# Scores of differential attention with keys as [high, low] on all 128 rows of TensorE

## The chip, the cores and the metric

The kernel runs on one core of a Trainium2 chip. The metric is the device time of one execution in microseconds (us), lower is better. Of the kernel before, three runs are shown: 2396.42, 2398.08 and 2400.06 us, median 2398.08 us. All matrix products are of float32 data; most are made as three products of `float32r` parts, a high part (the value rounded to that type) and a low part (what is left).

## The reference

One layer for a prompt of 1024 tokens with 16 meta tokens ahead of it, and for a sample of 8 streams of 16 new tokens each. A common in-projection feeds a retention branch (4 heads) and a differential attention branch (8 heads); both are gated and merged, and a feed-forward part with a final norm follows. What the change touches is the score product of the attention and the state update of the sample in the retention:

```python
def diff_softmax_mix(q, k, v, bias, mask, lam):
    s = jnp.einsum('bqhcd,bkhcd->bchqk', q, k) * (DIFF_DH ** -0.5) + bias
    s = jnp.where(mask, s, NEG_INF)
    p = jax.nn.softmax(s, axis=-1)
    a = p[:, 0] - lam * p[:, 1]
    return jnp.einsum('bhqk,bkhe->bqhe', a, v)
...
S_new = exp(lg * L) * Sf + jnp.einsum('bmhd,bmhe->bhde', kf * k_dec, vf)
```

Here `c` counts the two maps of a head, each with 64 channels (`DIFF_DH`), so that a score is a sum over 64 products.

## The kernel before, in words

**Stages.** A: norm, transposes and the first values (0 to about 45 us). B: retention, four heads, with dense products of the in-projection between its short products (to about 536 us). C: differential attention, eight heads, with the dense products of gates, of the next head's keys and queries, and at its end of the retention branch, between its short products (about 536 to 1280 us). D to F: the attention branch, the output projection and the feed-forward part (to the end at 2397 us).

**The scores (`scores`, L870 to L929).** For each block b of 128 queries and each of the two maps, the keys up to the block's end (144 to 1040 columns) are cut into one to three pieces. A piece is two products into one PSUM tile `psc` (two buffers, tag "m"): at L910 the queries `Q[:, m]` are the weights of 128 rows, 64 of the high part and 64 of the low part, against `K[:, m]`, which holds the high part of the keys twice; at L911 the 64 rows of the high queries alone stand against the 64 rows `KL` of the low keys. VectorE then adds the bias and takes the maximum in one instruction (L913), which frees the tile. So 224 pieces in all, 28 per head.

**Keys and queries (`task_kq`, L742 to L812).** For each head and each of three chunks of tokens ScalarE copies the keys out of PSUM (L754) and makes the two high halves (L755, L756); GpSimd copies each to the other 64 rows (L758, L759) and makes the low halves (L760, L762). Of the queries ScalarE makes the high halves (L781, L782) and VectorE the low ones (L785, L789) on the other 64 rows of the same tile.

**The sample's state (`load_kv` and L655 to L665).** For each retention head, eight products of 48 rows (16 tokens, three pairings of high and low) update the states of the streams; their operands come by DMA into `KV`.

**Order.** TensorE's program is written out by hand, and in stage C that of the other engines too. A planner (`Stream`, `weave`, `merge`) keeps a clock of TensorE's planned time: a short step is followed by dense steps of `C_RATIO` times its length; what other engines do is put into their program when the clock says that it should be ready (`LAT`), and a step that needs it waits by the clock ("at") while dense steps go on. The scores of a block wait for `rdy_kq`, which is set at L767 (keys: after four GpSimd steps of 1300 ns and 1500 ns) and L777 (queries: after 2200 ns). All DMAs go out on SyncE's queue.

Of the kernel before, what the change touches and what calls it, by code (L numbers as in the profile page):

```python
# [33 lines left out]
# of the 16 gate tiles, those computed beside heads 0..6 (the last stands beside head 7)  # L34
# [4 lines left out]
# ns that the other engines take, as the order of the program in attention supposes  # L39
T_LOAD, T_RAW = 3600, 5850  # L40
LAT = {
    "k": 1500, "kp": 1300, "q": 2200, "v": 6550, "max": 900, "exp": 900, "mix": 1300, "ah": 1050, "al": 1250,
# [4 lines left out]
# ns of two blocks' scores and of two blocks' values on TensorE  # L47
# [7 lines left out]
def nm(c):  # L55
    """Columns of chunk c without the meta tokens: (offset in the chunk, first, last of 1152)."""
    lo, hi = CH[c]
    o = NM if c == 0 else 0
    return o, lo + o - NM, hi - NM
# [3 lines left out]
def tile_kernel(ctx, tc, I, O):  # L63
# [41 lines left out]
    def rstd(small, ss, n, eps, name, mul=1.0):  # L105
        """(ss * mul + eps)^-0.5 on [:, n]; eps a number or a tile of the same shape."""
# [10 lines left out]
    class Stream:  # L117
        """Tasks (name, split, body) of dense products, issued step by step; a task's weights are asked for while
        the task before it runs. A step of 0 ns is one that has to wait for steps outside the stream.
        now is TensorE's time as far as the program stands. With defer, what another engine does at the end of  # L120
        a chain is put into the program only when the chain should have got there: each engine goes through its
        part of the program in order."""
# [47 lines left out]
        def run(self, ns):  # L170
            """Steps of ns in all, or as far as they go; the time they take."""
            done = 0
            while done < ns:
                t = self.step()
                if t == 0:
                    break
                done += t
            return done

        def until(self, name):  # L180
            """Through the end of the named task."""
            while self.name == name or any(n == name for n, _, _ in self.todo):
                t = self.step()
                assert t or self.name != name and all(n != name for n, _, _ in self.todo), (name, self.name)
# [3 lines left out]
    def split_w(pool_, src, name, sfx="", eng=None, raw_pool=None, wait=0):  # L188
        """A 4 KB-per-partition weight tile as two float32r parts."""
# [14 lines left out]
    # DRAM scratch  # L204
# [10 lines left out]
    # =====================================================================  # L215
    # In-projection: x^T in two float32r parts stays on chip
    # =====================================================================
# [7 lines left out]
    def tok_rows(b):  # L225
        """Block b: -1 is the meta tokens, 0..7 the prompt, 8 the sample; rows of x_all."""
# [7 lines left out]
    # Dense products run as one stream of tasks, split into steps of three matrix products, so that the  # L234
    # steps can stand between the short products of retention and attention. A step yields its time in ns.
    def dense_c(w, X, c, o, evac, name):
        """Chunk c of one 128-column tile of w^T x^T: evac(c, ps)."""
# [12 lines left out]
    def dense_x(w, evac, name, meta, ready=lambda c: True):  # L250
        """All of the tile, where ready(c) says that what the chunk overwrites has been read."""
# [5 lines left out]
    def dense_v(hs, evac, name):  # L257
        """256 columns of x @ w_in, tokens on partitions: evac(b, n, rows) per block."""
# [26 lines left out]
    def weave(main, ratio):  # L285
        """Steps of main with dense ones between them. Apart from its time, a step of main is ("at", t): wait
        until t by the stream's clock; or ("for", f): dense steps until f()."""
# [17 lines left out]
    def merge(*parts):  # L305
        """Steps of several parts (total ns, steps) side by side, each in its measure, those that wait behind."""
# [66 lines left out]
    # values of the attention heads 2r, 2r+1 (rows, as they are returned)  # L373
# [66 lines left out]
    # bytes of phase A go to what phase B writes late  # L440
# [5 lines left out]
    KV = pl.tile([3 * NQ, ND // 2, 384], R, name="KV", tag="kv")  # L446
# [13 lines left out]

    def side_tables():
        """Rows of the relative bias shifted by one per query, and lambda: for phase C."""
# [75 lines left out]
    def retention(r):  # L538
# [14 lines left out]
        def front(b):  # L553
            """The block's decayed scores, keys, values and queries, all but scores to come in two parts."""
# [35 lines left out]
        def load_kv(i):  # L590
            """Keys and values of four streams as 48 rows: [high, low, high] of the values, [high, high, low] of
            the keys."""
# [53 lines left out]
        # sample streams  # L646
# [24 lines left out]
    def gated(r):  # L671
        """Gated output of the head, transposed."""
# [52 lines left out]
    # the meta keys' 16 rows of probabilities and values: [high, low, high] and [high, high, low]  # L725
# [7 lines left out]
    Q = pc.tile([P, 2, NP], R, name="Q", tag="Q", bufs=1)  # L733
# [3 lines left out]
    # steps of a head that stand in the program: blocks of scores; "keys": the sample's keys are read  # L737
    seen = {h: set() for h in range(DH)}
    # its chunks of queries and keys that do
    done = {h: set() for h in range(DH)}  # L740

    def task_kq(h):  # L742
        def body_k(w):
            def evac_k(c, ps):
                if c == 0:
                    K = pc.tile([P, 2, NM + NP], R, name=f"K{h}", tag="K")
                    KL = pc.tile([P, NM + NP], R, name=f"KL{h}", tag="KL")
                    keys[h] = (K, KL)
                    load(KC[:, :, 0:PAST], I["cache_kT"][h])
                K, KL = keys[h]  # L750
# [7 lines left out]
                    lambda: nc.gpsimd.tensor_copy(K[64:128, 0, lo:hi], kf[0:64, lo:hi]),  # L758
                    lambda: nc.gpsimd.tensor_copy(K[0:64, 1, lo:hi], kf[64:128, lo:hi]),  # L759
                    lambda: nc.gpsimd.tensor_tensor(  # L760
                        KL[0:64, lo:hi], kf[0:64, lo:hi], K[0:64, 0, lo:hi].bitcast(F), op=ALU.subtract),
                    lambda: nc.gpsimd.tensor_tensor(  # L762
                        KL[64:128, lo:hi], kf[64:128, lo:hi], K[64:128, 1, lo:hi].bitcast(F), op=ALU.subtract),
# [3 lines left out]
                rdy_kq[h, "k", c] = G.now + 4 * LAT["kp"] + LAT["k"]  # L767
# [7 lines left out]
        def evac_q(c, ps):  # L775
# [5 lines left out]
            nc.scalar.activation(Q[0:64, 0, lo:hi], ps[0:64, :n], AF.Copy, scale=0.125)  # L781
            nc.scalar.activation(Q[64:128, 1, lo:hi], ps[64:128, :n], AF.Copy, scale=0.125)  # L782

            def low():
                nc.vector.scalar_tensor_tensor(  # L785
                    Q[64:128, 0, lo:hi], ps[0:64, :n], 0.125, Q[0:64, 0, lo:hi].bitcast(F),
                    op0=ALU.mult, op1=ALU.subtract,
                )
                nc.vector.scalar_tensor_tensor(  # L789
                    Q[0:64, 1, lo:hi], ps[64:128, :n], 0.125, Q[64:128, 1, lo:hi].bitcast(F),  # L790
                    op0=ALU.mult, op1=ALU.subtract,
                )
# [21 lines left out]
    def attention(h):  # L814
        """Steps of one head, by name."""
        at = {}

        def load_s():
            """Bias rows, and the sample's values and bias."""
# [18 lines left out]
        def load_v():  # L838
            """Values in two parts."""
# [693 lines left out]
```

## Time and profile before

| what | value |
|---|---|
| median of 3 runs (lowest to highest) | 2398.08 us (2396.42 to 2400.06) |
| span of the profiled execution, first to last instruction | 2397.1 us |
| mean granted TensorE clock over the span | 0.998 |
| TensorE busy | 2374.4 us (99%), 13738 products |
| VectorE, ScalarE, GpSimd busy | 969.0 (40%), 763.6 (32%), 496.3 us (21%) |
| DMA | 200 MB, 26% of the 16 engines' span |

The profiled execution has no time of its own beside its span; the span lies 1.0 us under the median of the runs. A product's row gives its start and a modelled duration in which neighbours overlap, so the time that a product takes from TensorE is read from its start to the start of the next one. Rows "PE" are products, "PEld" the loading of their weights; "64\*128" are the rows and columns of the array that a product uses, "64x392" the rows and columns of its moving operand.

### The profile page before, as it was taken

The numbers are of one execution on the slowest core, as the hardware profiler recorded it, in microseconds if no ns is written. First come the engines' busy times: TensorE is split into PE (matmuls) and PEld (weight loads), VectorE is DVE, ScalarE is ACT, GpSimd is POOL, SyncE is SP. The second block draws the span as 40 slices with busy tenths as digits, with TensorE's granted clock in tenths as the row PEclk, the third lists the DMA queues.
The fourth block names the chain that finished last, engine by engine and source line by source line (L and its number), as shares of the span: only waits on it lengthen the run. The fifth ranks groups of instructions, "written<-read, shape, count | busy, mean of one in ns | idle before, by whom it ended". The sixth has DMA issues, their size and how long they took to land.

```text
span 2397.1 us, 34595 instructions
## 1 busy us (share of the span) xinstructions
PE 2374.4 (99%) x13738; PEld 2188.1 (91%) x13738; DVE 969.0 (40%) x2246; ACT 763.6 (32%) x1756; POOL 496.3 (21%) x587
## 2 busy tenths in 40 slices
PE   8999999999999999999999999999999999999998
PEld 8999999998888888888889998899999999999987
DVE  5453333434445545545363333333233332333344
ACT  4223232224545545545464431121111111111112
POOL 1232222223223323322243320011000010000101
PEclk9999999999999999999999999999999999999999
DMA  5422323234222223223245643111101111011112
GB/s 207 133 82 78 99 69 102 80 114 113 81 75 87 74 75 88 73 75 99 65 135 172 223 143 108 49 31 59 44 27 44 45 53 41 31 45 45 53 36 88
DMA packets 129361, 200.00 MB, mean 83 GB/s; under 512 B 13432, under 2 KB 97656, under 8 KB 129200
## 3 DMA queue, kind: packets, MB, share of 16 engines
q1 hardware_dynamic: 129200, 197.80, 26.1%
q8 instruction: 108, 1.77, 0.3%
q14 instruction: 53, 0.43, 0.1%
HBM read 148.76 MB, written 53.78 MB: 84 GB/s over the span
## 4 chain that ended last, share of the span: by engine, by line
PE 94%; DVE 2%; DMA 1%; ACT 1%; issue 1%; POOL 0%; SPq 0%; DVEq 0%; POOLq 0%; ACTq 0%
PE pu L80 12%; PE pg L80 11%; PE pd L80 11%; PE ddk L80 5%; PE psc L80 5%; PE ddq L80 5%; PE dgr L80 4%; PE dgd L80 4%; PE drv L80 4%; PE ddv L80 4%; PE pdb L80 4%; PE pe L80 4%; PE drg L80 4%; PE po L80 3%; PE drb L80 3%; PE drk L80 2%
## 5 line engine op out<-in xcount | busy, mean ns | idle before, releaser
L1374 POOL TENSOR_TENSOR afl<-sgf,afh 128x384 fp32r<-128x384 f32 x66 | 69.7, 1056 | 730.2 <-ACT afh L1373 730.2
L913 DVE CUSTOM_DVE_ANT_0 E<-psc,TB 128x144 f32<-128x144 f32 (+6 forms) x224 | 114.1, 509 | 164.0 <-PE psc L80 159.2
L1391 DVE TENSOR_TENSOR H<-pd,H 128x512 f32<-128x512 f32 x198 | 135.7, 689 | 107.2 <-PE pd L80 107.2
L1289 ACT ACTIVATE sgf<-pg 128x384 f32<-128x384 f32 x66 | 32.3, 490 | 310.0 <-PE pg L80 310.0
L891 ACT ACTIVATE E<-E,ng 128x272 f32<-128x272 f32 (+7 forms) x128 | 101.0, 789 | 60.1 <-DVE ng L918 59.6
L1372 DVE TENSOR_TENSOR sgf<-pu,sgf 128x384 f32<-128x384 f32 x66 | 36.7, 556 | 164.9 <-PE pu L80 164.9
L80 PE MATMUL psc<-KL,Q 64*128 64x144 f32 (+6 forms) x224 | 93.5, 417 | 0.0
L80 PEld LDWEIGHTS psc<-KL,Q 64*128 64x128 f32 x224 | 40.9, 183 | 48.2 <-issue 43.0
L80 PE MATMUL psc<-K,Q 128*128 128x144 f32 (+6 forms) x224 | 74.1, 331 | 0.2
L1373 ACT CAST afh<-sgf 128x384 fp32r<-128x384 f32 x66 | 33.7, 511 | 116.8 <-DVE sgf L1372 116.8
L973 DVE TENSOR_TENSOR al<-pa,ah 128x512 fp32r<-128x512 f32 (+1 forms) x80 | 46.5, 581 | 49.1 <-ACT ah L972 48.5
L901 DVE SCALAR_TENSOR_TENSOR E<-E,rt,E 128x144 f32<-128x144 f32 (+3 forms) x64 | 54.9, 858 | 0.0
L563 POOL TENSOR_TENSOR v<-V,v 128x256 fp32r<-128x256 f32 x36 | 26.9, 748 | 113.2 <-ACT v L562 113.2
L972 ACT CAST ah<-pa 128x512 fp32r<-128x512 f32 (+1 forms) x80 | 40.1, 501 | 16.6 <-PE pa L961 16.3
L80 PEld LDWEIGHTS psc<-K,Q 128*128 128x128 f32 x224 | 42.1, 188 | 3.4 <-DVE mx L913 1.6
L961 PE MATMUL pa<-ident,E 128*128 128x128 f32 x288 | 44.5, 272 | 0.0
L1259 POOL TENSOR_TENSOR mt<-mt,gt 128x384 f32<-128x384 f32 x24 | 24.4, 1017 | 82.3 <-DVE gt L1258 72.9
L529 ACT COPY V<-drv 128x256 f32<-128x256 f32 x36 | 13.4, 372 | 83.7 <-PE drv L80 83.7
L856 POOL TENSOR_TENSOR VL<-VL,VH 128x512 fp32r<-128x512 f32 x16 | 20.3, 1292 | 88.6 <-ACT VH L855 88.6
L961 PEld LDWEIGHTS pa<-ident,E 128*128 128x128 f32 x288 | 35.5, 140 | 2.5
L80 PE MATMUL po<-ah,VH 128*128 128x256 f32 x128 | 37.5, 293 | 0.0
L785 DVE SCALAR_TENSOR_TENSOR Q<-ddq,Q 64x384 fp32r<-64x384 f32 (+1 forms) x24 | 12.2, 507 | 60.2 <-ACT Q L782 58.0
(1773 smaller groups left out, 8088.4 us busy)
## 6 DMA issues: line engine op xcount, KB each, us to landing
skd<-vecd SPq DMA_DIRECT2D x8, 584.0 KB, 14.1
out_k_t<-kf SPq DMA_DIRECT2D x8, 584.0 KB, 3.1
xt<-in_x_all SPq DMA_DIRECT2D x9, 512.0 KB, 5.4
vd<-v SPq DMA_DIRECT2D x36, 128.0 KB, 1.7
yr<-SG SPq DMA_DIRECT2D x24, 192.0 KB, 1.8
gd<-gdt SPq DMA_DIRECT2D x24, 192.0 KB, 1.8
gr<-grt SPq DMA_DIRECT2D x24, 192.0 KB, 1.8
YRL<-yr SPq DMA_DIRECT2D x12, 384.0 KB, 4.6
```

Source lines behind the costliest of these rows:

```text
L80: nc.tensor.matmul(out, l, r, start=start, stop=stop)
L891: nc.scalar.activation(E[m][:, :nk], E[m][:, :nk], AF.Exp, bias=ng[:, m : m + 1], accum_out=sm[:, m : m + 1])
L901: nc.vector.scalar_tensor_tensor(E[0][:, :nk], E[1][:, :nk], rt[:, 0:1], E[0][:, :nk], op0=ALU.mult, op1=ALU.add)
L913: nc.vector.tensor_tensor_reduce(out=E[m][:, k0:k1], in0=ps, in1=TB[:, u0 : u0 + k1 - k0], scale=1.0, scalar=-3e38, op0=ALU.add, op1=ALU.m ...
L961: nc.tensor.transpose(pt[:, o : o + P], blk[2 * g + j][:, NM + P * t : NM + P * (t + 1)], ident)
L972: nc.scalar.copy(ah[:, :o], pt[:, :o])
L973: G.later(LAT["ah"], lambda ah=ah, al=al, pt=pt, o=o: nc.vector.tensor_tensor(al[:, :o], pt[:, :o], ah[:, :o].bitcast(F), op=ALU.subtract))
L1289: nc.scalar.activation(sg[:, 384 * c : 384 * (c + 1)], ps, AF.Silu)
L1372: nc.vector.tensor_tensor(sg[:, cs], ps, sg[:, cs], op=ALU.mult)
L1373: nc.scalar.copy(ah[:, cs], sg[:, cs])
L1374: nc.gpsimd.tensor_tensor(al[:, cs], sg[:, cs], ah[:, cs].bitcast(F), op=ALU.subtract)
L1391: nc.vector.tensor_tensor(H[:, b, hs], ps, H[:, b, hs], op=ALU.add)
```

## The change

The keys of a map become one tile of 128 rows, 64 high and 64 low; the queries become two tiles, `QH` with the high part on both halves and `QL` with the low part on one half and zeros on the other. Both products of a piece then use 128 rows. The copies of the high keys on GpSimd go, copies of the high queries on GpSimd come. The 48-row products of the sample become 96-row products, of which rows 48 to 95 are zeros written once. Planned times of keys and queries change. Comments and docstrings are dropped (left out here).

```diff
-    "k": 1500, "kp": 1300, "q": 2200, "v": 6550, ...
+    "k": 1500, "kp": 1300, "q": 3600, "v": 6550, ...
...
-    KV = pl.tile([3 * NQ, ND // 2, 384], R, name="KV", tag="kv")
+    KV = pl.tile([96, ND // 2, 384], R, name="KV", tag="kv")
...
     nc.gpsimd.memset(QZ, 0.0)
+    for a in range(ND // 2):
+        nc.gpsimd.tensor_copy(KV[:, a, :], QZ[:96, :384])
...
-    Q = pc.tile([P, 2, NP], R, name="Q", tag="Q", bufs=1)
+    QH = pc.tile([P, 2, NP], R, name="QH", tag="QH", bufs=1)
+    QL = pc.tile([P, 2, NP], R, name="QL", tag="QL", bufs=1)
+    nc.vector.tensor_copy(QL[64:128, 0, :], AZ[64:128, :NP])
+    nc.vector.tensor_copy(QL[0:64, 1, :], AZ[0:64, :NP])
...
-                    K = pc.tile([P, 2, NM + NP], R, name=f"K{h}", tag="K")
-                    KL = pc.tile([P, NM + NP], R, name=f"KL{h}", tag="KL")
-                    keys[h] = (K, KL)
+                    keys[h] = pc.tile([P, 2, NM + NP], R, name=f"K{h}", tag="K")
...
                 fs = (
-                    lambda: nc.gpsimd.tensor_copy(K[64:128, 0, lo:hi], kf[0:64, lo:hi]),
-                    lambda: nc.gpsimd.tensor_copy(K[0:64, 1, lo:hi], kf[64:128, lo:hi]),
                     lambda: nc.gpsimd.tensor_tensor(
-                        KL[0:64, lo:hi], kf[0:64, lo:hi], K[0:64, 0, lo:hi].bitcast(F), op=ALU.subtract),
+                        K[64:128, 0, lo:hi], kf[0:64, lo:hi], K[0:64, 0, lo:hi].bitcast(F), op=ALU.subtract),
                     lambda: nc.gpsimd.tensor_tensor(
-                        KL[64:128, lo:hi], kf[64:128, lo:hi], K[64:128, 1, lo:hi].bitcast(F), op=ALU.subtract),
+                        K[0:64, 1, lo:hi], kf[64:128, lo:hi], K[64:128, 1, lo:hi].bitcast(F), op=ALU.subtract),
                 )
...
-                rdy_kq[h, "k", c] = G.now + 4 * LAT["kp"] + LAT["k"]
+                rdy_kq[h, "k", c] = G.now + 2 * LAT["kp"] + LAT["k"]
...
-            nc.scalar.activation(Q[0:64, 0, lo:hi], ps[0:64, :n], AF.Copy, scale=0.125)
-            nc.scalar.activation(Q[64:128, 1, lo:hi], ps[64:128, :n], AF.Copy, scale=0.125)
+            nc.scalar.activation(QH[0:64, 0, lo:hi], ps[0:64, :n], AF.Copy, scale=0.125)
+            nc.scalar.activation(QH[64:128, 1, lo:hi], ps[64:128, :n], AF.Copy, scale=0.125)
...
             def low():
-                nc.vector.scalar_tensor_tensor(
-                    Q[64:128, 0, lo:hi], ps[0:64, :n], 0.125, Q[0:64, 0, lo:hi].bitcast(F),
-                    op0=ALU.mult, op1=ALU.subtract,
-                )
...
+                for m in range(2):
+                    a, o = slice(64 * m, 64 * m + 64), slice(64 - 64 * m, 128 - 64 * m)
+                    nc.gpsimd.tensor_copy(QH[o, m, lo:hi], QH[a, m, lo:hi].bitcast(F))
+                    nc.vector.scalar_tensor_tensor(
+                        QL[a, m, lo:hi], ps[a, :n], 0.125, QH[a, m, lo:hi].bitcast(F),
+                        op0=ALU.mult, op1=ALU.subtract,
+                    )
...
-                    mm(ps, Q[:, m, qs], K[:, m, k0:k1], True, False)
-                    mm(ps, Q[hs, m, qs], KL[hs, k0:k1], False, True)
+                    mm(ps, QH[:, m, qs], K[:, m, k0:k1], True, False)
+                    mm(ps, QL[:, m, qs], K[:, m, k0:k1], False, True)
```

## Rows read from the trace of the kernel before

**Rows 1.** The page: TensorE's line of part 1, and part 4, the chain.

```profile
PE 2374.4 (99%) x13738; PEld 2188.1 (91%) x13738; DVE 969.0 (40%) x2246; ACT 763.6 (32%) x1756; POOL 496.3 (21%) x587
...
PE 94%; DVE 2%; DMA 1%; ACT 1%; issue 1%; POOL 0%; SPq 0%; DVEq 0%; POOLq 0%; ACTq 0%
```

**Rows 2.** Busy time by stretch: the attention, 560 to 1270 us.

```profile
560.00:1270.00 710.00, 706.05 (x3982) 610.99 (x3981) 357.07 (x1199) 354.24 (x919) 214.87 (x247) 1.00 0.27 83
```

**Rows 3.** Waits of PE, 536 to 1275 us: total us, times, longest.

```profile
PE pss L80 <- DVE mx L913: 2.5, 2, 1.4
```

**Rows 4.** Timeline of PE: first and last of 18 dense products.

```profile
864.97 0.33 PE L80 MATMUL dgd<-XH,wgd7h 128*128 128x384 f32 x1
...
867.92 0.34 PE L80 MATMUL dgd<-XH,wgd7l 128*128 128x384 f32 x1
```

**Rows 5.** Timeline of PE: a piece of 392 columns, two products behind.

```profile
860.43 0.34 PE L80 MATMUL psc<-K,Q 128*128 128x392 f32 x1
860.70 0.44 PE L80 MATMUL psc<-KL,Q 64*128 64x392 f32 x1
861.07 0.45 PE L80 MATMUL dgd<-XH,wgd7h 128*128 128x384 f32 x1
861.35 0.33 PE L80 MATMUL dgd<-XL,wgd7h 128*128 128x384 f32 x1
```

**Rows 6.** Timeline of PEld: the load for the product behind rows 5.

```profile
861.35 0.19 PEld L80 LDWEIGHTS dgd<-XH,wgd7l 128*128 128x128 f32 x1
```

**Rows 7.** Timeline of PE: a piece of 144 columns; eight other products of 144.

```profile
561.64 0.23 PE L80 MATMUL psc<-K,Q 128*128 128x144 f32 x1
...
562.34 0.34 PE L80 MATMUL dgd<-XL,wgd0h 128*128 128x384 f32 x1
...
845.12 1.15 PE L80 MATMUL pss<-KC,QZ 128*128 128x144 f32 x8
```

**Rows 8.** The page, part 5: the 64-row products and VectorE's reading of pieces.

```profile
L913 DVE CUSTOM_DVE_ANT_0 E<-psc,TB 128x144 f32<-128x144 f32 (+6 forms) x224 | 114.1, 509 | 164.0 <-PE psc L80 159.2
...
L80 PE MATMUL psc<-KL,Q 64*128 64x144 f32 (+6 forms) x224 | 93.5, 417 | 0.0
```

**Rows 9.** Tile KV (idle before: us, times); PE about one pair.

```profile
  issue: 3.5, 12
...
159.01 0.33 PE L80 MATMUL drk<-XH,wrk1l 128*128 128x384 f32 x1
159.27 0.50 PE L80 MATMUL pu_s<-KV 48*128 48x256 f32 x2
...
159.98 0.34 PE L80 MATMUL drk<-XL,wrk1h 128*128 128x384 f32 x1
```

**Rows 10.** Timeline of PE: a 96-row product and the product behind it.

```profile
699.39 0.28 PE L80 MATMUL po<-MA,VM 96*128 96x256 f32 x1
699.51 0.37 PE L80 MATMUL psc<-K,Q 128*128 128x456 f32 x1
```

**Rows 11.** Waits of DVE, 560 to 1270 us: total us, times, longest.

```profile
DVE E L913 <- PE psc L80: 159.2, 154, 3.6
```

**Rows 12.** Timeline at head 3's first queries: ACT, POOL, PE.

```profile
819.45 0.48 ACT L781 ACTIVATE Q<-ddq 64x384 fp32r<-64x384 f32 x1 [0.69 <-PE ddq L80]
...
820.25 0.74 POOL L762 TENSOR_TENSOR KL<-kf,K 64x256 fp32r<-64x256 f32 x1
821.06 1.28 POOL L197 TENSOR_TENSOR wgd6l<-wgd6w,wgd6h 128x512 fp32r<-128x512 f32 x1
...
821.38 0.23 PE L80 MATMUL psc<-K,Q 128*128 128x144 f32 x1
```

**Rows 13.** Key copies (ns: least, median, most); idle of POOL and DVE.

```profile
L758 POOL CAST K<-kf x24: 393/498/513, 544.6 to 1189.0; 64x400 fp32r<-64x400 f32 x8, 64x384 fp32r<-64x384 f32 x8, 64x256 fp32r<-64x256 f32 x8
...
6.01 0.56 POOL L114 TENSOR_TENSOR ra0r<-ra0t,mhalf 128x1 f32<-128x1 f32 x1 [3.72 <-DVE ra0t L110]
...
554.00 0.55 DVE L785 SCALAR_TENSOR_TENSOR Q<-ddq,Q 64x384 fp32r<-64x384 f32 x1 [16.52 <-ACT Q L782]
```

More of the change, by code (lines that the diff above doesn't have):

```diff
@@ L41 @@
 LAT = {
-    "k": 1500, "kp": 1300, "q": 2200, "v": 6550, "max": 900, "exp": 900, "mix": 1300, "ah": 1050, "al": 1250,
+    "k": 1500, "kp": 1300, "q": 3600, "v": 6550, "max": 900, "exp": 900, "mix": 1300, "ah": 1050, "al": 1250,
     "o": 700, "sq": 800, "rs": 1500, "two": 200, "yn": 900, "sexp": 2100, "smix": 1100, "sa": 2000, "w": 800,
@@ L745, in evac_k @@
                 if c == 0:
-                    K = pc.tile([P, 2, NM + NP], R, name=f"K{h}", tag="K")
-                    KL = pc.tile([P, NM + NP], R, name=f"KL{h}", tag="KL")
-                    keys[h] = (K, KL)
+                    keys[h] = pc.tile([P, 2, NM + NP], R, name=f"K{h}", tag="K")
                     load(KC[:, :, 0:PAST], I["cache_kT"][h])
-                K, KL = keys[h]
+                K = keys[h]
                 done[h].add(("k", c))
@@ L780, in evac_q @@
             n = hi - lo
-            nc.scalar.activation(Q[0:64, 0, lo:hi], ps[0:64, :n], AF.Copy, scale=0.125)
-            nc.scalar.activation(Q[64:128, 1, lo:hi], ps[64:128, :n], AF.Copy, scale=0.125)
+            nc.scalar.activation(QH[0:64, 0, lo:hi], ps[0:64, :n], AF.Copy, scale=0.125)
+            nc.scalar.activation(QH[64:128, 1, lo:hi], ps[64:128, :n], AF.Copy, scale=0.125)
             def low():
-                nc.vector.scalar_tensor_tensor(
-                    Q[64:128, 0, lo:hi], ps[0:64, :n], 0.125, Q[0:64, 0, lo:hi].bitcast(F),
-                    op0=ALU.mult, op1=ALU.subtract,
-                )
[L789 to L792, printed above, removed]
+                for m in range(2):
[5 more added lines that the diff above has]
+                    )
             G.later(LAT["ql"], low)
@@ L875, in scores @@
             yield ("at", max(rdy_kq[h, "q", cq], rdy_kq[h, "k", ck], mixed[-2]))
-            K, KL = keys[h]
+            K = keys[h]
             TB = at["s"][0]
@@ L905, in scores @@
             for m in range(2):
-                hs = slice(64 * m, 64 * m + 64)
                 for i in range(npc):
```

## The prediction

> **What bounds the kernel now.** I read the page first: TensorE is busy 99% of the span, and the chain that ended last runs on it for 94% [rows 1]. Then the stretch in which the change works: in the 710 us of the attention TensorE is busy 706 us, while VectorE and ScalarE are busy for half of it and GpSimd for 30% [rows 2]. Then its waits: the longest that the profile finds for TensorE there are two of 2.5 us in all, and not one before a score product [rows 3]. So the bound is the order of products on TensorE, and what counts is how far apart two products start, not how long a row says that one takes. The timeline gives that. In a run of dense products of 384 columns 17 steps take 2.95 us, 0.174 us each, or 0.453 ns per column [rows 4]; the weights of such a product take 0.19 us to load and are loaded beside the product ahead [rows 6], so that loading costs nothing there. The granted clock of the attention is 1.00, the higher of the two levels (2.4 GHz) [rows 2].
>
> The pieces of scores break this rhythm. About a piece of 392 columns the product with 128 rows starts at 860.43 [rows 5], the one with 64 rows 0.27 us later, the dense one behind it 0.37 us after that, and the next dense one only 0.28 us later. From 860.43 to 861.35 three products of 392, 392 and 384 columns take 0.92 us; at 0.453 ns per column they would take 0.53 us. So a piece loses **0.39 us**, some 0.1 at the step into the 64-row product, 0.2 at the step out of it, 0.1 at the step after. A piece of 144 columns [rows 7] takes 0.70 us to the second product behind it, where its columns would take 0.30: 0.40 us lost. The loss hangs on the change between 128 and 64 rows, not on the columns.
>
> **The change part by part.** *Score products.* There are 224 pieces [rows 8], as many products after as before, of the same columns, all with 128 rows. Nothing is left then that sets a score product apart from a dense one, so I take the whole 0.39 us as gained where a product's columns take longer than its weights' load. For the 16 pieces of 144 columns they don't: eight products of 144 columns with 128 rows take 0.12 us each ((1.15 - 0.29) / 7, with 0.29 for the modelled duration of one that stands alone) [rows 7], so such a piece would take 2 x 0.12 + 0.17 = 0.41 and gains 0.28 us. Sum: 208 x 0.39 + 16 x 0.28 = 81.1 + 4.5 = **85.6 us**.
>
> The nearest row for whether a zero-filled or wider product is as quick as a dense one is the 96-row product of the attention: the next product starts 0.12 us after it [rows 10], which is what 256 columns take at 0.453 ns, and no gap stands about it. So the limit lies between 64 and 96 rows.
>
> *Sample's products.* They have 48 rows and stand in 12 stretches, before each of which their load waited for nothing that the profile names [rows 9]. In the one shown four products of 384, 256, 256 and 384 columns take 0.97 us from 159.01 to 159.98, against 0.58 by columns: the same 0.39 us. With 96 rows they become like the product of the attention [rows 10]. Sum: 12 x 0.39 = **4.7 us**. All in all 90.3 us of TensorE's own time.
>
> *A rule that speaks against it.* The load shown runs from 861.35 to 861.54 [rows 6], beside a product that started at 861.35, with both on all 128 rows. The Trainium skill, "TensorE: Matmul & The Clock Gate", Part 3, "What overlaps and what doesn't", has loads overlap with products in flight only when their row groups differ. By that rule each second product of a piece would show its load of 0.19 us, 224 x 0.19 = 43 us, and the gain would be 48 instead of 90 us. The trace does not agree: dense steps of 0.174 us, shorter than the load, would not be possible. I keep 90.
>
> *What comes back: VectorE.* Each piece is read by one VectorE instruction of 0.51 us on average [rows 8], and only two tiles take turns. VectorE sat waiting for the piece in 154 of 224 cases [rows 11]; in the other 70 it came late already, busy with other work of its queue. There a quicker piece only meets a full tile sooner. Bounds: nothing comes back (the second tile takes it up, as it does now: no score product waits [rows 3]), or every one of the 70 gives its 0.39 back, 27 us. I take 10 us, nearer the lower end, because so far all 70 were taken up, and VectorE's load only goes from 50% to 357 / 622 = 57%.
>
> *Queries.* The copies of high keys (48 of 0.50 us [rows 13]) go from GpSimd, as many copies of high queries come: GpSimd's sum is unchanged, but the new ones stand on a tighter path. In head 3 the first queries leave PSUM at 819.45 and are used at 821.38, 1.93 us later [rows 12]; the last half of the keys' low part and a half of the next weights' low part (1.28 us) stand in GpSimd's queue just there. The planner now allows 3.6 instead of 2.2 us and puts dense steps between, which moves them and adds none. If a copy falls behind such a half, the first scores of heads 1 to 7 wait up to 1.3 us each: between 0 and 9 us. I take 1, for the 1.4 us more that the plan allows cover one half. The later chunks have the same allowance with other scores to go on with. Behind the waiting copies on GpSimd stand the next gate's low halves, which the plan needs only one task later. VectorE's two instructions per chunk stay, and so do all DMAs on SyncE's queue.
>
> *Zeros.* Four copies into `KV` on GpSimd, 0.5 us each by the nearest row, 2 us; if they are put at the start, they lie in GpSimd's idle time of 3.7 us before the first norm [rows 13]; without that cover they would cost at most their 2 us. Two copies into `QL` on VectorE lie in its idle 16.5 us before the first low queries [rows 13]. Both are costed at nothing. Keys ready 2.6 us earlier by plan: nothing, dense steps fill that time either way.
>
> **Sum.** Span 2397.1 - 85.6 - 4.7 + 10 + 1 = 2317.8 us. The runs' median lies 1.0 us above that span, so the forecast is **2319 us**.
>
> **The rivals.** (1) *The other engines take over in the attention.* All 70 late pieces give back their gain and the queries cost 9 us: 2398 - 90.3 + 27.3 + 9 = 2344 us. For it: the order was fitted to scores that take 0.7 us where the plan counts 0.29, so true waits had slack that nobody planned. Against it: half-empty engines and no wait of a score product today [rows 2, 3]. Chance 0.14.
>
> (2) *Nothing changes, since rows don't set the price.* If the loss came from changing the weights between two products on one PSUM tile, a 128-row pair would pay it too, and the time would stay at 2398 us, within 0.2%. Against it: the pair of 48-row products, other tiles and another stage, loses the same 0.39 us, and the 96-row product loses none [rows 9, 10]. Chance 0.04. The Trainium skill, in the page named above, Part 3, has a product of few rows take the same time as one of 128; by it the time would stay as it is. The rows show that the steps around it don't.
>
> (3) *Slower: the queries' copies on GpSimd.* Place: the queue in which the 48 new copies stand, two per chunk, behind the low halves of weights. Price: it turns the result around once each of the 24 chunks makes TensorE wait over 90.3 / 24 = 3.8 us, three halves of 1.28 us in front of each. At 5 us per chunk it would be 2398 - 90 + 120 = 2428 us. For it: first queries are used 1.9 us after they leave PSUM [rows 12]. Against it: GpSimd is busy 30% [rows 2], and each task brings only two halves. Chance 0.03.
>
> **How the numbers follow.** The forecast has 0.79. Its own bounds: 2305 (nothing comes back, and 0.01 us of rounding on each of 224 pieces) to 2335 (all 27 us come back). The range holds it and reaches a little into rival 1: 2304 to 2338 us. A difference of 0.2% (5 us) is about what a measurement of this kernel can tell from no change. Forecast and rival 1 are faster: 0.93; rival 2 the same: 0.04; rival 3 slower: 0.03.
>
> **What would show it.** No product with 64\*128 or 48\*128 rows is left; about a score product of 392 columns starts stand 0.17 to 0.18 us apart, and the dense product behind is followed after 0.174 us. The stretch from the first to the last score shrinks by 70 to 85 us, the rest hardly. Waits of score products for VectorE's reading appear, 5 to 15 us in all; waits of TensorE for `QH` by GpSimd stay under 3 us. My argument falls if second products start more than 0.25 us after first ones of 392 columns, if waits in the attention sum to over 30 us, or if the retention stage gets longer through the zeros in `KV`.

## The result and the profile after

The changed kernel takes 2326.73 us (median of 4 runs, 2324.53 to 2330.18) against 2399.07 us before (2396.42 to 2401.50): a ratio of 0.9704, 95% interval 0.9690 to 0.9717, so about 3% faster. That is inside the range, 8 us above the forecast of 2319. The profiled execution has a span of 2325.0 us, 72.1 less than before.

The page of the changed kernel, the engines of part 1 and the chain of part 4, against [rows 1]:

```profile
PE 2288.9 (98%) x13738; PEld 2186.9 (94%) x13738; DVE 968.5 (42%) x2248; ACT 762.6 (33%) x1756; POOL 502.9 (22%) x591
...
PE 90%; DVE 4%; DMA 2%; ACT 2%; issue 1%; POOL 1%; SPq 0%; DVEq 0%; POOLq 0%; ACTq 0%
```

The stretch from the first to the last score product of the changed kernel, busy times by stretch (columns as in [rows 2]: stretch, its length, then PE, PEld, DVE, ACT and POOL busy, granted clock, DMA share, GB/s):

```profile
556.30:1193.00 636.70, 619.28 (x3955) 604.04 (x3955) 355.61 (x1192) 350.93 (x913) 216.40 (x248) 1.00 0.31 92
```

The same stretch of the kernel before, which the document has not shown yet:

```profile
561.60:1266.20 704.60, 700.65 (x3952) 605.80 (x3950) 355.55 (x1192) 352.20 (x913) 214.18 (x246) 1.00 0.27 83
```

The products are as many as before, and the loads of weights as long (604 and 606 us); what went is the time between products. The stretch is 67.9 us shorter. TensorE's idle time in it grew from 704.6 - 700.7 = 3.9 to 636.7 - 619.3 = 17.4 us.

The timeline of PE in the changed kernel about a piece of 392 columns, which answers to [rows 5]:

```profile
754.90 0.34 PE L80 MATMUL psc<-K,QH 128*128 128x392 f32 x1
755.08 0.34 PE L80 MATMUL psc<-K,QL 128*128 128x392 f32 x1
755.26 0.34 PE L80 MATMUL dgd<-XH,wgd5h 128*128 128x384 f32 x1
755.43 0.34 PE L80 MATMUL dgd<-XL,wgd5h 128*128 128x384 f32 x1
```

The load of the next weights there, timeline of PEld, which answers to [rows 6]:

```profile
755.08 0.19 PEld L80 LDWEIGHTS dgd<-XH,wgd5h 128*128 128x128 f32 x1
```

Three products take 0.53 us where they took 0.92: 0.39 us gained, and the steps are those of dense products, 0.18, 0.18 and 0.17 us. The load of 0.19 us runs beside the product that starts with it.

What came back is in the changed kernel's waits of TensorE, 531 to 1275 us (total us, times, longest), against [rows 3]:

```profile
PE psc L80 <- DVE mx L915: 5.2, 10, 1.8
PE pss L80 <- DVE mx L915: 4.6, 2, 2.6
PE drb L80 <- DVE rbt L1164: 3.2, 1, 3.2
PE pyt L1034 <- DVE yn L1013: 2.2, 1, 2.2
PE po L80 <- DVE al L975: 1.7, 6, 0.8
PE psc L80 <- POOL QH L791: 1.4, 2, 1.0
```

The wait of `drb` lies behind the last score product, the others between the first and the last. VectorE's waits, as in [rows 11]:

```profile
DVE E L915 <- PE psc L80: 106.3, 107, 3.8
```

VectorE now waits for a piece 107 times instead of 154, so it comes late to 117 of 224 pieces. One of these waits, which returns in each of heads 2 to 6, first in the timeline of PE:

```profile
801.73 0.28 PE L80 MATMUL psc<-K,QL 128*128 128x264 f32 x1
802.40 0.36 PE L80 MATMUL psc<-K,QH 128*128 128x264 f32 x1 [0.39 <-DVE mx L915]
```

And in that of DVE:

```profile
801.81 0.43 DVE L915 CUSTOM_DVE_ANT_0 E<-psc,TB 128x264 f32<-128x264 f32 x1 [0.31 <-PE psc L80]
802.17 0.08 DVE L915 DVE_READ_ACCUMULATOR2_ANT mx<- 128x1 f32 x1
```

Two pieces of one block follow each other with nothing dense between; the third piece has to wait for the first to be read. The row counts 0.39 us, but from start to start it is 0.67 where 264 columns take 0.12: about 0.16 us of each wait hide in the modelled duration of the product ahead.

### The profile page after: what moved, and what is told of

The parts are those of the page before. It is cut to its first block, busy times and chain, and to the rows that moved or that the text cites. A ratio compares the mean times of both kernels' runs of the same rounds, so it can differ in the third digit from the quotient of the medians.

```text
span 2325.0 us, 34635 instructions
## 1 busy us (share of the span) xinstructions
PE 2288.9 (98%) x13738; PEld 2186.9 (94%) x13738; DVE 968.5 (42%) x2248; ACT 762.6 (33%) x1756; POOL 502.9 (22%) x591
## 4 chain that ended last, share of the span: by engine, by line
PE 90%; DVE 4%; DMA 2%; ACT 2%; issue 1%; POOL 1%; SPq 0%; DVEq 0%; POOLq 0%; ACTq 0%
PE pu L80 12%; PE pg L80 12%; PE pd L80 11%; PE ddv L80 4%; PE ddk L80 4%; PE pdb L80 4%; PE pe L80 4%; PE drv L80 4%; PE dgd L80 4%; PE dgr L80 4%; PE drg L80 4%; PE ddq L80 3%; PE po L80 3%; PE psc L80 3%; PE drb L80 3%; PE drk L80 2%
## 5 line engine op out<-in xcount | busy, mean ns | idle before, releaser
L80 PE MATMUL psc<-K,QH 128*128 128x144 f32 (+6 forms) x224 | 73.3, 330 | 6.9 <-DVE mx L915 5.2
L80 PE MATMUL psc<-K,QL 128*128 128x144 f32 (+6 forms) x224 | 71.1, 319 | 0.0
L80 PEld LDWEIGHTS psc<-K,QH 128*128 128x128 f32 x224 | 42.2, 188 | 10.4 <-issue 5.5
L792 DVE SCALAR_TENSOR_TENSOR QL<-ddq,QH 64x384 fp32r<-64x384 f32 (+1 forms) x48 | 24.5, 510 | 57.5 <-ACT QH L786 54.9
L80 PEld LDWEIGHTS psc<-K,QL 128*128 128x128 f32 x224 | 42.3, 189 | 0.0
L80 PE MATMUL po<-al,VH 128*128 128x256 f32 x128 | 36.4, 284 | 1.8 <-DVE al L975 1.7
L620 POOL TENSOR_TENSOR Sp<-S,Sp 128x256 fp32r<-128x256 f32 x32 | 23.9, 747 | 60.1 <-ACT Sp L619 52.2
```

The source lines that it names most:

```text
L80: nc.tensor.matmul(out, l, r, start=start, stop=stop)
```

## The experiments

The kernel before ran beside each of these kernels, with a median of 2398.3 to 2398.9 us.

**1. Only the rows.** The changed kernel, with the second product on the 64 rows that hold something.

```diff
-                    mm(ps, QL[:, m, qs], K[:, m, k0:k1], False, True)
+                    hs = slice(64 * m, 64 * m + 64)
+                    mm(ps, QL[hs, m, qs], K[hs, m, k0:k1], False, True)
```

> The changed kernel, but the second product of each piece of scores uses the 64 rows that hold something (low queries against high keys); the zero rows of the queries stay in their tile unused. Theory (the change between 128 and 64 rows on TensorE costs 0.39 us per piece): the gap comes back about all 224 pieces, the 18 us that were given back in the attention go again, and the time is 2390 to 2400 us. Rival (the gain comes from the new layout of keys and queries, their fewer key copies and the new planned times, all of which stay here): 2325 to 2335 us. About a piece of 392 columns the starts should stand 0.27, 0.37 and 0.28 us apart by the theory, 0.18 each by the rival.

Measured: 2403.1 us, ratio 1.0023 (1.0013 to 1.0033). A piece of 392 columns, timeline of PE:

```profile
867.30 0.34 PE L80 MATMUL psc<-K,QH 128*128 128x392 f32 x1
867.57 0.44 PE L80 MATMUL psc<-K,QL 64*128 64x392 f32 x1
867.94 0.44 PE L80 MATMUL dgd<-XH,wgd7h 128*128 128x384 f32 x1
868.22 0.34 PE L80 MATMUL dgd<-XL,wgd7h 128*128 128x384 f32 x1
```

The starts stand 0.27, 0.37 and 0.28 us apart again, and the whole gain is gone: rows alone make it, and the rival falls. The time is 3 us above the range that was expected, and even above the kernel before. The stretch of the scores shows why:

```profile
555.90:1269.00 713.10, 703.55 (x3955) 608.61 (x3954) 356.07 (x1192) 352.67 (x913) 215.74 (x248) 1.00 0.27 83
```

It is 713.1 us, 8.5 more than before at the same price per product, with 9.5 us idle instead of 3.9. Of the 8.5 us some 1.7 are granted clock: it was 0.51 at 1202.2 to 1205.5 us and 0.50 at 1219.2 to 1222.4 us, where the kernel before has one such stretch among its scores (0.50 at 575.0 to 578.2 us), and one more at half rate for about 3.4 us loses half of that. So the new layout and its plan have a cost of their own, before any piece gets quicker.

**2. The sample's products back on 48 rows,** all else as changed.

```diff
-    KV = pl.tile([96, ND // 2, 384], R, name="KV", tag="kv")
+    KV = pl.tile([48, ND // 2, 384], R, name="KV", tag="kv")
...
-    for a in range(ND // 2):
-        nc.gpsimd.tensor_copy(KV[:, a, :], QZ[:96, :384])
```

> The changed kernel with the sample's state products back on 48 rows and without the zero rows. Theory: 12 stretches lose 0.39 us each, the first score product starts 4.7 us later than with the change (560.8 instead of 556.1 us), and the span is about 2329.7 us. Rival (the zero rows and their four copies on GpSimd cost as much as they save): the first score product stays within 1 us of 556.1 us.

Measured: first score product at 561.8 us, one run of 2338.9 us, span 2337.1. The start is 5.5 us later than with the change, but 1.5 of these are there before the first such product (159.4 against 157.9 us), so some 4.0 belong to it. That is near the theory; the rival falls. The span is 7 us above what was expected. The mean granted clock accounts for that much (span and clock of the core). With the change:

```profile
core 0: 2325.0 us, clock 0.998
```

In this run:

```profile
core 0: 2337.1 us, clock 0.994
```

At half rate for a share of the time the loss is (1 - clock) x span: 4.7 and 14.0 us. More of this run went at the lower level. Two of its stretches at that level stand behind waits that the changed kernel has as well (see the last section), so nothing shows the edit to be the reason.

**3. Where the limit lies.** The changed kernel with 48, 64, 72 and 96 rows in the four heads.

```diff
-                    mm(pu[...], KV[:, a + j, :P], KV[:, a + j, P:], True, True)
+                    n = (48, 64, 72, 96)[r]
+                    mm(pu[...], KV[:n, a + j, :P], KV[:n, a + j, P:], True, True)
```

> The changed kernel with the sample's state products on 48, 64, 72 and 96 rows in retention heads 0, 1, 2 and 3 (the rows beyond 48 are zeros). Theory (two ways of using the array, up to 64 rows and above): heads 0 and 1 lose about 0.39 us per stretch of such products, heads 2 and 3 nothing. Rival (the price falls with the rows that are left empty): 0.39, 0.25, 0.2 and 0 us.

Measured: 2327.2 us in one run. The timeline of PE in this run about a pair with 64 rows, then with 72:

```profile
276.47 0.34 PE L80 MATMUL drk<-XH,wrk2l 128*128 128x400 f32 x1
276.75 0.50 PE L80 MATMUL pu_s<-KV 64*128 64x256 f32 x2
277.18 0.45 PE L80 MATMUL drk<-XH,wrk2h 128*128 128x400 f32 x1
277.46 0.34 PE L80 MATMUL drk<-XL,wrk2h 128*128 128x400 f32 x1
...
402.61 0.34 PE L80 MATMUL drk<-XH,wrk3l 128*128 128x400 f32 x1
402.79 0.40 PE L80 MATMUL pu_s<-KV 72*128 72x256 f32 x2
403.04 0.35 PE L80 MATMUL drk<-XH,wrk3h 128*128 128x400 f32 x1
403.22 0.34 PE L80 MATMUL drk<-XL,wrk3h 128*128 128x400 f32 x1
```

From the first to the last row of each: 0.99 us with 64 rows, 0.61 with 72, where columns alone take 0.59. So there are two kinds of product, up to 64 rows and from 72 at the latest; how many rows stay empty does not matter. The graded rival falls.

**4. Product or way into it.** The kernel before, with the products of two pieces regrouped.

```diff
-                for i in range(npc):
+                for i0 in range(0, npc, 2):
+                    part = []
+                    for i in range(i0, min(npc, i0 + 2)):
...
                         mm(ps, Q[:, m, qs], K[:, m, k0:k1], True, False)
-                    mm(ps, Q[hs, m, qs], KL[hs, k0:k1], False, True)
+                        part.append((i, k0, k1, ps))
+                    for i, k0, k1, ps in part:
+                        mm(ps, Q[hs, m, qs], KL[hs, k0:k1], False, True)
```

> The kernel before, with the 128-row products of two pieces of a map put ahead of their two 64-row products, so that 20 of a head's 28 pieces share the way into 64 rows and back. Theory (the price is for going over, not for the product): two pieces together lose 0.39 us instead of 0.78, and between the two 64-row products starts stand as far apart as their columns take (0.18 us for 392). Rival (each 64-row product is slow by itself): two pieces lose 0.6 us or more. The time itself is not clear beforehand, as both tiles of scores are then filled at once and VectorE empties them late: 2370 to 2400 us.

Measured: 2382.0 us in one run. Two pieces of 392 columns, timeline of PE:

```profile
856.51 0.52 PE L80 MATMUL psc<-K,Q 128*128 128x392 f32 x2
856.96 0.62 PE L80 MATMUL psc<-KL,Q 64*128 64x392 f32 x2
857.51 0.44 PE L80 MATMUL dgd<-XH,wgd7h 128*128 128x384 f32 x1
857.79 0.34 PE L80 MATMUL dgd<-XL,wgd7h 128*128 128x384 f32 x1
```

Five products take 1.28 us where their columns take 4 x 0.178 + 0.174 = 0.89: 0.39 us lost for two pieces, not 0.78. One expected sign did not come: the second 64-row product starts at 857.25, 0.29 us behind the first, not 0.18. The dense product behind the way back shows the same, 0.28 us to its next one: the first step behind each going over is 0.1 us longer than the columns, and that is part of the 0.39. Whether further steps are slow is shown by the kernel before, where four of the sample's products of 48 rows follow each other:

```profile
285.82 0.34 PE L80 MATMUL drk<-XH,wrk2l 128*128 128x384 f32 x1
286.09 0.74 PE L80 MATMUL pu_s<-KV 48*128 48x256 f32 x4
287.04 0.34 PE L80 MATMUL drk<-XL,wrk2h 128*128 128x384 f32 x1
```

From 285.82 to 287.04 these four and the two dense products about them take 1.22 us, where columns alone take 0.81: four lose 0.41 us together, as much as one or two. The price is for going over to 64 rows and back, and a product of few rows is not slow by itself; the rival falls.

From the first to the last score product this run takes 688.6 us, 16 less than the kernel before, of the 31 us that 80 ways saved would give. About 7 of the other 15 are granted clock, which was 0.50 at 639.5 to 646.0 and at 663.5 to 670.0 us. TensorE's waits grew by 4.6 us, most of it two waits of score products for VectorE (2.4 and 2.1 us) to empty a tile. The rest is not accounted for.

**5. The queries' plan back to 2200 ns.**

```diff
-    "k": 1500, "kp": 1300, "q": 3600, ...
+    "k": 1500, "kp": 1300, "q": 2200, ...
```

> The changed kernel with the planned time of the queries back at 2200 ns (3600 with the change). In the run with 64 rows and the new layout the attention took 713.1 us from first to last score product, 8.5 more than before the change, though every product cost the same: some of what was given back is not VectorE's lateness but the new layout and plan. Theory (the longer plan of the queries shifts the other engines' order, so that the low part of the retention rows stands ahead of a small norm step on GpSimd at the end of head 6, with 2.2 us of waiting there): this wait goes, waits of score products for the copies of high queries rise from 1.4 to 3 to 7 us, and the time stays within 2320 to 2332 us. Rival (the copies on GpSimd need the longer plan): waits for QH above 9 us and a time of 2333 us or more.

Measured: 2327.0 us, ratio 0.9701 (0.9687 to 0.9716). The wait of 2.2 us at the end of head 6 went, waits of score products for VectorE fell from 5.2 to 1.2 us, those for `QH` rose from 1.4 to 4.0 us: as the theory had it, and no gain in sum.

**6. High queries by ScalarE** straight from PSUM, plan at 2200 ns.

```diff
+            nc.scalar.activation(QH[64:128, 0, lo:hi], ps[0:64, :n], AF.Copy, scale=0.125)
+            nc.scalar.activation(QH[0:64, 1, lo:hi], ps[64:128, :n], AF.Copy, scale=0.125)
...
-                    nc.gpsimd.tensor_copy(QH[o, m, lo:hi], QH[a, m, lo:hi].bitcast(F))
```

> The changed kernel with the other half of the high queries written by ScalarE straight from PSUM, instead of copied by GpSimd, and the planned time of queries at 2200 ns. Theory (the copies in GpSimd's queue and the shifted order are the layout's cost): no wait of TensorE for QH by GpSimd, no 2.2 us wait at the end of head 6, 2316 to 2324 us. Rival (all that came back is VectorE late at its two score tiles, and ScalarE's 48 more instructions of 0.48 us make its queue later still): 2326 to 2335 us.

Measured: 2330.5 us, ratio 0.9713 (0.9697 to 0.9729). No wait for `QH` by GpSimd is left, but waits of score products for ScalarE (2.3 us, 5 times) and VectorE (5.8 us, 8 times) stand there instead. My theory's time was missed; the rival's range holds it.

**7. Three tiles for scores,** two for transposes.

```diff
-    NB = {"dq": 2, "tr": 3, "m": 2, "o": 1}
+    NB = {"dq": 2, "tr": 2, "m": 3, "o": 1}
```

> The changed kernel with three PSUM tiles for scores and two, not three, for transposes. Theory (score products wait because VectorE is late at two tiles): their 5.2 us of waits for VectorE and the 4.6 us of the sample's scores mostly go; what the missing transpose tile costs instead is open, waits of pa, pot or pyt for ScalarE or VectorE. If these stay under 5 us, the time is 2316 to 2323 us; else it is above 2325 us. Rival (VectorE is late for another reason, and a third tile only moves the wait to the next product): waits of score products stay above 4 us.

Measured: 2352.7 us in one run. The score products' waits for VectorE fell to 2.7 us and those of the sample's scores for it went, so the rival (above 4 us) falls; transposes now wait 15.2 us (`pa`) and 8.6 us (`pm`) for the low part on VectorE. With only two transpose tiles the question what a third score tile alone would give stays open.

**8. More distance for the values' low part.**

```diff
-    ... "ah": 1050, "al": 1250,
+    ... "ah": 1050, "al": 1750,
```

> The changed kernel with the planned time of the low part of the probabilities at 1750 instead of 1250 ns, which puts 0.5 us more of dense steps ahead of the values' products. Theory (the quicker pieces took the slack out of short steps that the plan sets too close): the six waits of the values' products for VectorE (1.7 us counted, some 0.35 us each from start to start) go, and the time is 2 to 4 us less, 2322 to 2325 us. Rival (the wait moves to the next product that needs VectorE): 2326 to 2328 us with as much waiting in all.

Measured: 2341.1 us in one run, 14 more than the change and worse than either side expected. The waits aimed at fell to 0.2 us; those of score products for VectorE rose to 12.1 us (10 times, the longest 2.6), those of `pyt` to 5.8.

**9. Experiment 1 with the old plan:** 64 rows, the new layout, planned times as before the change.

```diff
-    "k": 1500, "kp": 1300, "q": 3600, ...
+    "k": 1500, "kp": 1300, "q": 2200, ...
...
-                rdy_kq[h, "k", c] = G.now + 2 * LAT["kp"] + LAT["k"]
+                rdy_kq[h, "k", c] = G.now + 4 * LAT["kp"] + LAT["k"]
```

> The run with 64 rows and the new layout of keys and queries, with the planned times of keys and queries as they were before the change (keys after four GpSimd steps, queries after 2200 ns). That run took 8.5 us more in the attention than the kernel before, at the same price per product. Theory (the new planned times shifted the other engines' order): first to last score product within 704 to 708 us, and 2396 to 2400 us in all. Rival (the copies of high queries on GpSimd are late, whatever the plan): 711 to 717 us, with waits for QH of 4 us or more, and 2400 to 2405 us.

Measured: 2400.0 us, ratio 1.0007 (0.9998 to 1.0017); 712.0 us from first to last score. The time lies where both sides end, the stretch where only the rival is. Its row in the waits of PE in this run:

```profile
PE psc L80 <- POOL QH L791: 4.0, 2, 2.0
```

What stands before the second of them, timeline of POOL:

```profile
1188.34 1.26 POOL L197 TENSOR_TENSOR wgr7l<-wgr7w,wgr7h 128x512 fp32r<-128x512 f32 x1 [3.81 <-issue]
1189.66 1.06 POOL L791 CAST QH<-QH 64x384 fp32r<-64x384 f32 x2
```

And the score product that waits, timeline of PE:

```profile
1190.21 0.33 PE L80 MATMUL psc<-K,QH 128*128 128x144 f32 x1 [2.01 <-POOL QH L791]
```

The copies stand behind a half of the next weights' low part, the place that rival 3 named. GpSimd sat idle for 3.81 us ahead of that half: ScalarE finished the last high queries of the chunk at 1187.13 us and made the weights' high part only after them, until 1188.20, and the copies stood behind the half that needed it. My theory that the plan alone is the layout's cost falls: with the old plan it is two waits of 2.0 us for these copies, with the new plan 1.4 us of them and 3.4 us (1.9 and 1.5) where the shifted order makes VectorE late. The 7.4 us that this stretch is longer than before are these 4.0 and some 3.4 of granted clock (last section).

**10. The change with the old plan** with 128 rows.

```diff
-    "k": 1500, "kp": 1300, "q": 3600, ...
+    "k": 1500, "kp": 1300, "q": 2200, ...
...
-                rdy_kq[h, "k", c] = G.now + 2 * LAT["kp"] + LAT["k"]
+                rdy_kq[h, "k", c] = G.now + 4 * LAT["kp"] + LAT["k"]
```

> The changed kernel with the planned times of keys and queries as they were before the change. Theory (order): the 2.2 us wait at the end of head 6 goes as with 2200 ns alone; first to last score product is 630 to 636 us, the time 2320 to 2326 us. Rival (late copies): waits for QH of 4 us or more, as with 2200 ns alone, and 2326 to 2330 us.

Measured: 2326.3 us, ratio 0.9698 (0.9683 to 0.9712), with 4.0 us of waits for `QH` and 1.2 for VectorE at the scores, as in 5. The first score product starts at 559.2 and the last at 1194.3 us: these 635.1 us lie where the theory had them, the time and the waits where the rival had them. The two plans are equal within what can be measured.

**11. 150 ns more per piece in the planner's count.**

```diff
+PLAN = 150
...
-                    yield max(220, 2 * (k1 - k0) / 2.36)
+                    yield max(220, 2 * (k1 - k0) / 2.36) + PLAN
```

> The changed kernel with 150 ns more per piece in the planner's count, which puts some 0.25 us more of dense steps behind each piece and moves the clock on, nearer to the spacing that the slow pieces had before the change. Theory (the quicker pieces come too close for VectorE): waits of score products for VectorE fall from 5.2 to under 2.5 us and those of the values' products for the low part go, 2318 to 2325 us. Rival (dense steps that are spent early are missing later in the head): waits elsewhere grow by as much or more, 2326 to 2340 us.

Measured: 2350.8 us in one run; score products wait 12.7 us (18 times) for VectorE.

**12. Another ratio in the planner.**

```diff
-C_RATIO = 1.68
+C_RATIO = 1.8
```

> The changed kernel with 1.8 instead of 1.68 times its length in dense steps behind each short step. Theory (spacing): some 2 to 6 us less, 2320 to 2325 us. Rival (the order is fitted, and any shift of it moves the waits rather than removing them, as the longer plan of the low part did with 14 us): 2326 to 2345 us.

Measured: 2338.5 us in one run; `pyt` waits 10.3 us (11 times) for VectorE. In 12 the rival holds; in 11 the time lies on the rival's side but 11 us above its range, and the waits at which the edit aimed grew themselves. Dense steps between the pieces are no cure here. That the order of the other engines was fitted to the old spacing, so that each shift makes them late elsewhere, fits 8, 11 and 12, but no run tests it by itself. None of the runs beats the changed kernel beyond its interval.

## Why the prediction was right, point by point

**The score products.** Right in cause and size. The sum took 0.39 us for 208 pieces; the timelines show 0.39 for 392 columns, and over all 32 pieces of that width the loss is 0.39 to 0.40 us before and at most 0.02 after but for one. The cause is shown from three sides: rows alone bring the loss back (1), the limit lies between 64 and 72 rows (3), and two pieces that share the way lose it once (4). Rival 2 is out. What it takes from the Trainium skill, that a product of few rows takes as long as one of 128, stands in "TensorE: Matmul & The Clock Gate" under "Why this matters for your kernels", not in Part 3. The trace agrees for the product itself, since four in a row lose no more than one (0.41 us, experiment 4); the loss lies in the steps into and out of them. The rule by which loads would have shown is out too: with every product on 128 rows the load of 0.19 us stands beside a product in flight, and steps are 0.18 us. The Trainium skill, "TensorEngine Tiling (Array Packing)", "Key Properties", says that going over to another tiling mode drains TensorE; the trace agrees with 0.39 us for both ways together.

Loads do show at the going over, which the prediction left out. Timeline of PEld in the kernel before, about the piece of [rows 5]:

```profile
860.70 0.18 PEld L80 LDWEIGHTS psc<-KL,Q 64*128 64x128 f32 x1 [0.25 <-issue]
861.07 0.19 PEld L80 LDWEIGHTS dgd<-XH,wgd7h 128*128 128x128 f32 x1 [0.19 <-issue]
```

The load for a dense product starts one product ahead of it [rows 6]. These two start only with the product that needs them, after 0.25 and 0.19 us without a load. The page, part 5, has all 224 such loads (busy us, mean ns, then the idle time ahead of them), before and after:

```profile
L80 PEld LDWEIGHTS psc<-KL,Q 64*128 64x128 f32 x224 | 40.9, 183 | 48.2 <-issue 43.0
L80 PEld LDWEIGHTS psc<-K,QL 128*128 128x128 f32 x224 | 42.3, 189 | 0.0
```

Two loads that no product covers would be 0.18 + 0.19 = 0.37 us, close to the 0.39 that is lost. That the loss is made of these loads is argued from the rows; no run tells it from another cost of going over.

**The sample's products.** 4.7 us forecast. The first score product starts 561.64 - 556.29 = 5.35 us earlier, of which 159.27 - 157.86 = 1.4 us are gained before the first such product; a part of that stretch, in retention, had a mean granted clock of 0.98 before and 1.00 after. That is a chance of the run and no work of the change: in experiments 5 and 10, whose kernels keep the change's zeros and 96 rows, it was 0.98 again. Busy times by stretch of the kernel before:

```profile
45.00:128.00 83.00, 81.51 (x546) 77.45 (x545) 32.22 (x74) 21.66 (x56) 16.71 (x23) 0.98 0.39 120
```

Of the changed kernel:

```profile
45.00:128.00 83.00, 81.51 (x557) 77.50 (x557) 32.27 (x75) 22.79 (x59) 17.59 (x25) 1.00 0.39 120
```

So 3.9 us are the edit's. In two of the 12 stretches the products still start late (in the first head the four of the second half at 164.31, 0.42 us after the product ahead at 163.89), so that some of their 0.39 is not won.

**What came back.** Forecast 10 us by VectorE and 1 by the queries, measured 85.6 - 67.9 = 17.7 us. This is the term that was mis-sized. The profile counts 17.4 - 3.9 = 13.5 us of it as idle time. Some 3 us more hide in modelled durations, since TensorE waits for more than 0.05 us 26 times in the stretch instead of 7 times, with about 0.16 us hidden in each. The granted clock has no part in it: it was 0.50 once among the scores before (575.0 to 578.2 us) and once after (568.0 to 571.2 us).

Experiment 1 splits it. At the old pace of pieces 8.5 us came with the layout and its plan; less the 1.7 us of clock, which the changed kernel does not have, 6.8. The other 10.9 came with the quicker pieces. The second part is what I had for VectorE, 10 us, and the profile shows it there: late for 117 pieces instead of 70, idle time of TensorE up from 9.5 to 17.4 us, of it 3.7 at score products (1.5 to 5.2) and 2.0 at the sample's scores (2.6 to 4.6). The first part is what I had at 1 us, "for the 1.4 us more that the plan allows cover one half": they do, waits for `QH` are 1.4 us, but with the shift by those 1.4 us a step of the retention rows stands ahead of a small norm step on GpSimd. Timeline of POOL in the changed kernel:

```profile
1145.12 1.83 POOL L1138 TENSOR_TENSOR YRL<-YRL,YRH 128x768 fp32r<-128x768 f32 x1 [1.74 <-ACT YRH L1137]
1146.90 0.70 POOL L114 TENSOR_TENSOR rn63r<-rn63t,mhalf 128x2 f32<-128x2 f32 x1
```

In the kernel before the norm step comes first, at 1214.25, and the rows' step at 1218.32 us. The changed order made TensorE wait 1.9 us in experiment 1 (2.2 with the change), and there was another wait of 1.5 us for VectorE; without the shift (9) the copies cost 4.0 us. I had weighed the move against its own consumer only, not against what follows in the fitted order. In 1 and 9 a lower granted clock behind such waits added 1.7 and 3.4 us to it.

**Costed at nothing.** The `KV` zeros were not written at the start, as I had supposed, but at 40.9 to 43.3 us, beside GpSimd's idle time; `QL`'s zeros took 2 x 0.69 us at 533.6 us on VectorE, which then waited 13.7 us for the first queries. The end of the kernel behind the last score product is 1.1 us longer (1132.0 against 1130.9 us): TensorE waits 3.2 us there for VectorE's `rbt`, which it did not before [rows 3], and the clock behind it was 0.50 at 1247.3 to 1250.5 us; part of that is won back by other steps.

**The sum.** -85.6 + 17.7 for the scores, -3.9 for the sample, -1.4 by the clock in retention, +1.1 at the end: -72.1 us, as the spans have it. The forecast had -79.3, and 6.7 of the 7.2 us between them are what came back.

**The signs.** No product of 64\*128 or 48\*128 is left, steps about a score product of 392 columns are 0.17 to 0.18 us, score products wait 5.2 us for VectorE and 1.4 us for `QH`, retention is not longer, and waits in the attention stay under 30 us, all as put down. One sign was missed: the stretch shrank by 67.9 us, not by 70 to 85. VectorE's share came to 355.6 / 636.7 = 56%, near the 57% forecast (the 622 us in that division come from no sum; 710 - 85.6 = 624 gives the same share).

## What to carry to other kernels

Read what a product costs from the starts of its neighbours: a 64-row product among 128-row ones loses 0.39 us here that stands in no row's duration, and zero rows beside the data take it away for the price of writing them once. Where the order cannot be changed, put short-row products together, since the price is for the way in and out. When a step that sets the pace gets quicker, expect some of the gain back in a program whose order was made for the slow step (here a fifth of it), and weigh a shift in a planned order by all that stands behind it, not by its own consumer.

## What the runs showed of the hardware that had not been expected

The granted clock falls for a while behind some short waits and not behind others. In the run of experiment 9 TensorE waited 2.01 us at 1190 us, and 1192 to 1202 us then went at 0.50, the lower of the two levels (1.2 GHz). In experiment 2 the waits of 1.8 us at the scores and 1.9 us at `pyt` were followed by such stretches too; with the change itself the same two waits, 1.8 and 2.2 us, were not. Busy times and granted clock by stretch, of experiment 9:

```profile
1192.00:1202.00 10.00, 10.00 (x27) 8.05 (x27) 5.38 (x23) 3.88 (x12) 1.08 (x3) 0.50 0.18 52
```

Of experiment 2:

```profile
1141.70:1145.00 3.30, 3.30 (x12) 3.30 (x12) 1.09 (x4) 2.36 (x8) 0.91 (x3) 0.50 0.00 0
1158.70:1162.00 3.30, 3.30 (x14) 3.20 (x13) 1.55 (x3) 1.61 (x3) 0.47 (x1) 0.50 0.67 191
```

Of the changed kernel, behind the same two waits:

```profile
1132.00:1136.00 4.00, 3.27 (x20) 3.31 (x21) 2.97 (x15) 2.84 (x8) 2.84 (x3) 1.00 0.01 4
1149.00:1153.00 4.00, 4.00 (x28) 3.93 (x28) 1.71 (x4) 2.23 (x4) 1.67 (x1) 1.00 0.46 123
```

So a wait of about 2 us on TensorE can cost more than itself. Runs of one and the same kernel differ by it: of the ten of experiment 1 those at a mean clock of 0.997 took 2401.0 to 2403.0 us and the one at 0.993 took 2408.7, so a single run of a kernel with such waits tells little about a difference of a few us. What decides between the two cases was not tried.
